# Two-layer diffusion backbone on one core: four outputs advance side by side over the k tiles at the start of each stage, and the second half's norm sums stand further on in PE's order

## The chip, the cores and the metric

One core of a Trainium2 chip runs the whole program in one launch. The metric is the device time of one execution in microseconds (us). A time is given as the median of several runs; a profile belongs to one execution and has that execution's own time.

## The reference

A trunk of two layers works on 512 latent tokens and 256 context tokens, 1024 channels each, in f32. Each layer is a half-step SwiGLU FFN, a token mixer, and another half-step FFN, and ahead of each stands a modulated RMS norm. Cut to what matters here:

```python
def rmsnorm(x, g):
    return x * lax.rsqrt(jnp.mean(x * x, axis=-1, keepdims=True) + EPS) * g
...
for l in range(DEPTH):                       # 2
    x = x + 0.5 * gate * ((silu(h @ wg) * (h @ wu)) @ wd)      # h = rmsnorm(x) * (1 + scale) + shift
    hx, hc = modulate(rmsnorm(x, ...)), modulate(rmsnorm(ctx, ...))
    yx, yc = even_mixer(hx, hc, ...) if l % 2 == 0 else odd_mixer(hx, hc, ...)
    x = x + mx[5] * yx
    x = x + 0.5 * gate * ((silu(h @ wg) * (h @ wu)) @ wd)
return rmsnorm(x, final_norm_g)
```

`shift`, `scale` and `gate` come from `silu(c) @ ada_w + ada_b`. The even mixer is a gated MLP beside windowed attention; the odd mixer is a convolution and a bidirectional recurrence with sigmoid gates.

## The kernel before, in words

**Layout.** Channels lie on the partitions, in 8 tiles of 128 ("the k tiles"), and the 768 tokens (256 context, then 512 latent) are columns. They are handled in two halves of 384 columns, TA (0 to 384) and TB (384 to 768); the last FFN has only latent tokens, in two halves XA and XB of 256. A weight is split into a high and a low part, and so is the normed input (`H`, tiles `hhi` and `hlo`): one product of f32 accuracy is three matmuls (`mm3`, L118). An output tile of 128 channels therefore costs 8 x 3 = 24 matmuls into one of 8 PSUM banks (`bank`, L105).

**A stage boundary.** The last thing that a stage does is to update X, channel tile by channel tile, first for TA and then for TB (`down` in `ffn`, L676, or `project_out`, L865). For each tile `Norm.add` (L548) squares the new X on ACT and DVE adds it to a sum (`flush`, L561). When all eight are in, `Norm.run` (L607) sets three things on a planner's clock: `stats` (L566, three matmuls with a column of ones, then a reciprocal square root of 13 small DVE instructions), then `spread` (L582, three matmuls that spread the result over the partitions), then for each k tile `apply` (L587: DVE multiplies, ACT adds the shift and writes `hhi`) and `halve` (L594: DVE writes `hlo`). PE's first products of the next stage read `hhi` and `hlo` of TA.

**The planner.** `Clock` (L72) is not the chip's time. Every `mm` adds an estimate to `clk.t` (L116: 173.5 ns for 384 columns), and `clk.tick()` after each `mm3` emits whatever has fallen due. So "2500 ns after" means "after the next 15 products in the program". The program order is then a priority: the framework issues an engine's instructions in that order when their inputs are expected, and may let a later one pass an earlier one that is not ready.

```python
        def run(self, after=2500.0):
            self.left = DK
            self.flush()
            clk.at(after, self._stats)

        def _stats(self):
            self.stats()
            self.prep_mod()
            clk.at(3600.0, self._spread)
```

`ready` (L624) runs the planner forward until all `halve` of a half have been emitted.

**The first products of a stage.** They go output by output, each over all 8 k tiles:

- `ffn`, `gate_up` (L653) for the first pair (p = 0): gate and up of f = 0, then of f = 1, for TA, and then the same for TB. In the first FFN the TA half is made earlier, in the start-up code (`pre`, L1389).
- `even_mixer`, `project_in` (L930): six outputs (two of k and v, four of q) for TA, called at L1127; those for TB are fillers between attention units.
- `odd_mixer`, `xx_mm` (L1257): four outputs for TA (L1356), then one of TB ahead of each `conv` (L1359).

Between stages weights are brought in by chunks (`Chunk`, L164): a DMA of 1 MB, a copy on ACT and a subtraction on DVE per tile (L189, L192; L219 and L236 in the FFNs that use a seven-product scheme). `stream["limit"]` bounds how many of the 12 weight tiles are planned at once; it is 8 from the end of an FFN until the second half's last `halve` (L603). In three FFNs DVE then forms sums of the `H` tiles (`form`, L701, `last_form`, L718) that the seven-product scheme reads from p = 2 (or 4) on.

**The modulation.** `ada_step` (L508) is a background job on DVE that multiplies `ada_w` with the condition. `ada_event` (L512) emits one step of it every 900 ns of the planner's clock until `mods[0][2]` is done, then less often. The end of one modulation is a small matmul on PE (`finish`, L463).

Of the kernel before, what the change touches and what calls it, by code (L numbers as in the profile page):

```python
# [89 lines left out]
def hybrid_kernel(ctx: ExitStack, tc: tile.TileContext, a: dict, out: bass.AP):  # L90
# [27 lines left out]
    def mm3(o, w, x, start, stop, again=False):  # L118

        mm(o, w[0], x[0], start, False, again=again)  # L120
        mm(o, w[0], x[1], False, False, again=again)
        mm(o, w[1], x[0], False, stop, again=again)
        clk.tick()

    def split(hi, lo, src, src_hi=None):
        act.activation(hi, src if src_hi is None else src_hi, AF.Copy)  # L126
# [385 lines left out]
    def ada_event():  # L512
        if bg["on"] and not (bg["sums"] and mods_done.get((0, 2), 0) == 4):
            ada_step()
        if not bg["over"]:
            clk.at(900.0 if mods_done.get((0, 2), 0) < 4 else bg["every"], ada_event)

    def mod(l, m):
        while mods_done.get((l, m), 0) < 4:
# [16 lines left out]
    class Norm:  # L536
# [67 lines left out]
                    stream["limit"] = SLOTS  # L604
                    pump()

        def run(self, after=2500.0):  # L607

            self.left = DK
            self.flush()  # L610
            clk.at(after, self._stats)

        def _stats(self):
            self.stats()
            self.prep_mod()
            clk.at(3600.0, self._spread)

        def _spread(self):
            self.spread()
# [23 lines left out]
    def ffn(l, j, halves, before, nxt, reserve=(), pre={}):  # L643
# [7 lines left out]
        with tc.tile_pool(name=f"ffn{l}{j}", bufs=4) as fp:  # L651

            def gate_up(p, spans, G):  # L653
                wg, wu = gu[p]
                need(wg)
                need(wu)
                for c0, c1 in spans:
                    n = c1 - c0
                    ready(c1, before)
                    if p == SEVEN.get((l, j), 99) - 2 and c1 == c_hi:  # L660
                        plan_forms(form, 4000.0 if p == 0 else 8000.0)
                    for f in (p, p + 1):
                        o = (f - p) * 128
                        made = (c0, f, 0) in pre
                        pg, pu = (pre[c0, f, i] if made else bank("pgu") for i in range(2))
                        for ps, w in ((pg, wg), (pu, wu)):
                            for k in range(0 if made else DK):
                                mm3(ps[:, 0:n], w.w(k, o, o + 128), (hi[k][:, c0:c1], lo[k][:, c0:c1]), k == 0, k == DK - 1)
                            if ps is pg:
                                s = temp("silu")[:, 0:n]  # L670
                                act.activation(s, pg[:, 0:n], AF.Silu)
                        g = temp("g")[:, 0:n]
                        dve.tensor_tensor(g, pu[:, 0:n], s, op=ALU.mult)
                        split(G[f][0][:, c0:c1], G[f][1][:, c0:c1], g)
# [211 lines left out]
    def even_mixer(before):  # L886
        hi, lo = H
        xd = dp.tile([128, 8, NT], F32, name="xd")
        with ExitStack() as es:
# [37 lines left out]
                return q_tiles[i // 2][:, i % 2]  # L927


            def project_in(i, c0, c1):  # L930
                ch = (ckv, cq[0], cq[1])[i // 2]
                need(ch)
                ps = bank()
                for k in range(DK):
                    w = ch.w(k, (i % 2) * 128, (i % 2) * 128 + 128)
                    mm3(ps[:, 0:c1 - c0], w, (hi[k][:, c0:c1], lo[k][:, c0:c1]), k == 0, k == DK - 1)
                act.copy(KV[:, i, c0:c1] if i < 2 else Q(i - 2)[:, c0:c1], ps[:, 0:c1 - c0])

            def rope(src):
                s_hi, s_lo = tr("sh", 2), tr("sl", 2)  # L940
# [182 lines left out]
                                      w[r, 0:256].rearrange("p (h t) -> p h t", h=2), op=ALU.mult)  # L1123

            ready(TA[1], before)
            for i in range(6):
                project_in(i, *TA)  # L1127
            kv = xp.tile([128, 4, NT], F32R, tag="x", name="kv")
            spare = xp.tile([128, 4, NT], F32R, tag="x", name="spare")
            keys(0, 2)  # L1130
# [24 lines left out]
            def fill_in(i):  # L1155

                if i < 6:
                    ready(NT, before)
                    project_in(i, *TB)
                    if i % 2:  # L1160
                        if i == 5:
                            stream["limit"] = SLOTS - 3
                        done((ckv, cq[0], cq[1])[i // 2])
                if i == 1:
                    rope(KV[:, 0, NCTX:])
                    keys(2, 6)
                elif i == 2:
                    values(3, 6)
                elif i > 2:
                    rope(Q(i - 3)[:, NCTX:])  # L1170
# [48 lines left out]
    def odd_mixer(before):  # L1219
# [4 lines left out]
        with tc.tile_pool(name="odd", bufs=1) as op:  # L1224
# [29 lines left out]
                area["xc"] = xp.tile([128, 4, NT], F32, tag="x", name="xc")  # L1254
                area["t0"] = xp.tile([128, 4, NT], F32, tag="x", name="t0")

            def xx_mm(k, c0, c1):  # L1257
                ch = cxx[k // 2]
                ready(c1, before)
                need(ch)  # L1260
                o = k % 2 * 128
                ps = xps[k, c0] = bank()
                for kk in range(DK):
                    mm3(ps[:, 0:384], ch.w(kk, o, o + 128), (hi[kk][:, c0:c1], lo[kk][:, c0:c1]), kk == 0, kk == DK - 1)
                if k % 2 and c0:
                    done(ch)

            def conv(k):

# [83 lines left out]
                gelu2(v, ps, 512)  # L1353
                combine(k, v)

            for k in range(4):  # L1356
                xx_mm(k, *TA)
            take()
            for k in range(4):  # L1359
                xx_mm(k, *TB)  # L1360
                conv(k)
                if k == 1:
                    halve_next(0)
            for k in range(8):
                do_rg(k)
                for kind, n in ODD_FILL[k]:
                    if kind == "xx":
                        xx_mm(n, *TA)
                        xx_mm(n, *TB)
                        conv(n)  # L1370
                    else:
                        do_gx(n)
# [189 lines left out]
```

## Time and profile before

| what | value |
|---|---|
| median of 3 runs | 2581.3 us (2578.44 to 2583.24) |
| the profiled execution's own time | 2580.57 us |
| its span, first to last instruction | 2578.8 us |
| mean granted TensorE clock | 0.988 |
| PE busy | 2522.0 us (98%) |
| DVE busy | 1883.5 us (73%) |
| ACT busy | 1247.0 us (48%) |

A row of the profile has a start and a duration in us from the span's start; "x24" counts instructions; square brackets give the idle time of the engine just before and what ended it. `ps<-hhi,w` reads "writes tile ps from hhi and w". The granted clock is 1.00 at 2.4 GHz and 0.50 at 1.2 GHz.

### The profile page before, as it was taken

To read this page: it belongs to the slowest core of one execution; us is meant where nothing else is said; L and a number is where in the kernel's file an instruction comes from. 1 tells how busy PE (TensorE), PEld (TensorE's weight loads), DVE (VectorE), ACT (ScalarE), POOL (GpSimd) and SP (SyncE) were. 2 spreads that over 40 slices of the span, in tenths; PEclk is the share of its full clock that TensorE was granted. 3 is DMA by queue.
4 is the path that set the end of the run, shared out by engine and by line. 5 is a ranking of instruction groups with operands and counts; after the bars stand their busy time and mean duration, and the time that the engine had idled before them with its cause. 6 is when DMAs were issued, how large, how long until landed. Compare 5 with 4: busy or idle time off the path is not lost.

```text
span 2578.8 us, 37727 instructions
## 1 busy us (share of the span) xinstructions
PE 2522.0 (98%) x14370; PEld 2354.4 (91%) x14370; DVE 1883.5 (73%) x3680; ACT 1247.0 (48%) x2433; POOL 210.2 (8%) x269
## 2 busy tenths in 40 slices
PE   8999999999999999999999999999999999999998
PEld 5999999998899999999899899999999989988887
DVE  7888977776879897786776988765468898644444
ACT  3344444445556354444454444444545996423322
POOL 0022012200000002201220021021200000000000
PEclk9999999999999999999999999999999999999999
DMA  9357558552112516645664176664642123322221
GB/s 329 107 139 180 146 133 207 144 164 93 34 58 56 184 57 156 175 121 136 166 169 151 46 186 170 200 148 106 139 131 82 51 81 104 110 98 98 90 90 58
DMA packets 248429, 328.45 MB, mean 127 GB/s; under 512 B 19984, under 2 KB 172728, under 8 KB 247736
## 3 DMA queue, kind: packets, MB, share of 16 engines
q1 hardware_dynamic: 213264, 278.69, 33.2%
q0 software_dynamic: 34560, 47.20, 12.1%
q8 instruction: 112, 1.84, 0.3%
q14 instruction: 69, 0.57, 0.1%
q10 hardware_dynamic: 424, 0.15, 0.0%
HBM read 262.04 MB, written 63.96 MB: 126 GB/s over the span
## 4 chain that ended last, share of the span: by engine, by line
PE 88%; DVE 6%; ACT 3%; DMA 2%; issue 1%; SPq 0%; ACTq 0%; DVEq 0%
PE pd L112 26%; PE pgu L112 25%; PE seeded L112 18%; PE ps L112 11%; PE po L112 4%; PE pv L112 2%; PE sc L112 1%; PE pt L1101 1%; PE sl L112 1%; DVE w L192 1%; PE pre L112 1%; DMA raw<-in_ffn_w_down_dram 1%; ACT w L189 1%; DVE hlo L598 0%; DMA fw<-in_ada_w_dram 0%
## 5 line engine op out<-in xcount | busy, mean ns | idle before, releaser
L112 PE MATMUL pd<-ghi,w 128*128 128x256 f32 (+2 forms) x2528 | 644.6, 342 | 2.1 <-ACT ghi L126 2.0
L112 PE MATMUL pgu<-hhi,w 128*128 128x384 f32 (+2 forms) x2144 | 596.1, 350 | 0.9 <-ACT hhi L592 0.6
L112 PEld LDWEIGHTS pd<-ghi,w 128*128 128x128 f32 x2528 | 439.3, 188 | 53.8 <-ACT ghi L126 4.9
L112 PE MATMUL pd<-glo,w 128*128 128x512 f32 (+2 forms) x1264 | 430.9, 342 | 0.2 <-DVE glo L127 0.2
L112 PEld LDWEIGHTS pgu<-hhi,w 128*128 128x128 f32 x2144 | 393.6, 189 | 27.9 <-ACT hhi L592 1.3
L112 PE MATMUL pgu<-hlo,w 128*128 128x384 f32 (+2 forms) x1072 | 375.1, 350 | 1.3 <-DVE hlo L598 1.2
L687 POOL DMA_DIRECT2D kept<-add x240 | 208.6, 905 | 1649.8 <-ACT add L686 1640.1
L192 DVE TENSOR_TENSOR w<-raw,w 128x512 fp32r<-128x512 f32 x404 | 271.3, 688 | 94.3 <-ACT w L189 91.6
L189 ACT ACTIVATE w<-raw 128x512 fp32r<-128x512 f32 x404 | 245.1, 626 | 176.5 <-PE pd L112 74.2
L487 DVE SCALAR_TENSOR_TENSOR acc<-aw,cs,acc 128x512 f32<-128x512 f32 x392 | 279.9, 746 | 46.0 <-DMA aw<-in_ada_w_dram 45.2
L219 DVE TENSOR_TENSOR w<-raw,w 128x512 fp32r<-128x512 f32 x348 | 232.9, 688 | 105.1 <-ACT w L236 101.2
L112 PE MATMUL seeded<-form,w 128*128 128x384 f32 x1392 | 263.0, 336 | 3.7 <-ACT seeded L780 2.6
L112 PEld LDWEIGHTS pd<-glo,w 128*128 128x128 f32 x1264 | 237.7, 188 | 27.0 <-DVE glo L127 2.7
L686 ACT ACTIVATE add<-pd,gate 128x256 f32<-128x256 f32 x240 | 138.8, 581 | 247.0 <-PE pd L112 226.6
L112 PE MATMUL seeded<-hhi,w 128*128 128x384 f32 x928 | 247.7, 335 | 1.5 <-ACT hhi L126 1.0
L112 PEld LDWEIGHTS seeded<-form,w 128*128 128x128 f32 x1392 | 244.0, 188 | 4.9 <-ACT seeded L780 2.9
L236 ACT ACTIVATE w<-raw 128x512 fp32r<-128x512 f32 x348 | 207.8, 626 | 59.9 <-DVE raw L235 18.9
L112 PEld LDWEIGHTS pgu<-hlo,w 128*128 128x128 f32 x1072 | 203.0, 189 | 15.1 <-DVE hlo L598 2.1
L112 PE MATMUL ps<-hhi,w 128*128 128x384 f32 (+1 forms) x704 | 198.4, 356 | 4.5 <-ACT t L1317 3.2
L112 PEld LDWEIGHTS seeded<-hhi,w 128*128 128x128 f32 x928 | 168.6, 188 | 3.4 <-ACT hhi L126 2.5
L112 PE MATMUL seeded<-hlo,w 128*128 128x384 f32 x464 | 155.3, 335 | 0.4 <-DVE hlo L127 0.4
L112 PEld LDWEIGHTS ps<-hhi,w 128*128 128x128 f32 x704 | 133.2, 194 | 11.6 <-ACT t L1317 3.8
(300 smaller groups left out, 3635.5 us busy)
## 6 DMA issues: line engine op xcount, KB each, us to landing
aw<-in_ada_w_dram SPq DMA_DIRECT2D x128, 512.0 KB, 5.2
raw<-in_ffn_w_gate_dram SPq DMA_DIRECT2D x44, 1024.0 KB, 5.4
raw<-in_ffn_w_up_dram SPq DMA_DIRECT2D x44, 1024.0 KB, 5.3
raw<-in_ffn_w_down_dram SPq DMA_DIRECT2D x40, 1024.0 KB, 5.1
kept<-add POOLq DMA_DIRECT2D x120, 256.0 KB, 5.3
kept<-add POOLq DMA_DIRECT2D x120, 128.0 KB, 5.3
x<-kept SPq DMA_DIRECT2D x48, 192.0 KB, 4.3
fw<-in_ada_w_dram SPq DMA_DIRECT2D x16, 512.0 KB, 8.8
```

The lines of the kernel that those rows point to most:

```text
L112: pe.matmul(o, w, x, start=start, stop=stop, skip_group_check=again)
L189: act.activation(tiles[i][:, 0:512], self.raw[:, i * 512:i * 512 + 512], AF.Copy)
L192: dve.tensor_tensor(t[:, 512:1024], self.raw[:, i * 512 - 512:i * 512], t[:, 0:512].bitcast(F32), op=ALU.subtract)
L219: dve.tensor_tensor(l, src[key], h.bitcast(F32), op=ALU.subtract)
L236: act.activation(halves_of(key)[0], src[key], AF.Copy)
L487: dve.scalar_tensor_tensor(acc[:, v, :], w[:, k, :], s, acc[:, v, :], op0=ALU.mult, op1=ALU.add)
L686: act.activation(t, ps[:, 0:c1 - c0], AF.Copy, scale=state["gate"][:, 4 * c + d, v:v + 1])
L687: pool.dma_start(out=saved(l, j)[:, 4 * c + d, c0:c1], in_=t, accum_op=ALU.add)
L1101: pe.transpose(ps[:, o:o + 128], self.src[hh][b + bb], ident)
```

## The change

The program has a new helper, `side_by_side`, which takes several outputs and loops over the k tiles outside and over the outputs inside. It is used for the first products of each stage: in the FFNs for the four outputs of p = 0, for each half that was not made in the start-up code; in the even mixer for the first four and then the last two outputs of TA; in the odd mixer for the four of TA and then for pairs of TB. So `conv(0)` comes after two outputs of TB. The number of products, their operands and each bank's order over k stay as they were.

`Norm.run` has other distances for the second half: `stats` after 5500 ns (3500 ns where a half is 256 wide) in place of 2500, and `spread` 3000 ns after that in place of 3600. The first half keeps its distances. `ada_event` has 800 ns in place of 900. In the even mixer the limit on weight tiles is raised after the first four outputs.

```diff
+    def side_by_side(parts, n, c0, c1):
+
+        for k in range(DK):
+            for o, w in parts:
+                mm3(o[:, 0:n], w(k), (H[0][k][:, c0:c1], H[1][k][:, c0:c1]), k == 0, k == DK - 1)
...
-            clk.at(900.0 if mods_done.get((0, 2), 0) < 4 else bg["every"], ada_event)
+            clk.at(800.0 if mods_done.get((0, 2), 0) < 4 else bg["every"], ada_event)
...
-        def run(self, after=2500.0):
+        def run(self):
...
-            clk.at(after, self._stats)
+            clk.at(2500.0 if self.c1 < NT else 5500.0 if self.n == 384 else 3500.0, self._stats)
...
-            clk.at(3600.0, self._spread)
+            clk.at(3600.0 if self.c1 < NT else 3000.0, self._spread)
...
+                    four = {}
+                    if p == 0 and (c0, p, 0) not in pre:
+                        four = {(f, i): bank("pgu") for f in (0, 1) for i in range(2)}
+                        side_by_side([(ps, lambda k, f=f, i=i: (wg, wu)[i].w(k, f * 128, f * 128 + 128)) for (f, i), ps in four.items()], n, c0, c1)
                     for f in (p, p + 1):
                         o = (f - p) * 128
-                        made = (c0, f, 0) in pre
-                        pg, pu = (pre[c0, f, i] if made else bank("pgu") for i in range(2))
+                        made = p == 0
+                        pg, pu = (pre[c0, f, i] if (c0, f, i) in pre else four[f, i] if four else bank("pgu") for i in range(2))
...
-            def project_in(i, c0, c1):
-                ch = (ckv, cq[0], cq[1])[i // 2]
-                need(ch)
-                ps = bank()
-                for k in range(DK):
...
+            def project_in(tiles, c0, c1):
+                pss, parts = {}, []
+                for i in tiles:
...
+                side_by_side(parts, c1 - c0, c0, c1)
+                for i, ps in pss.items():
+                    act.copy(KV[:, i, c0:c1] if i < 2 else Q(i - 2)[:, c0:c1], ps[:, 0:c1 - c0])
...
-            for i in range(6):
-                project_in(i, *TA)
+            project_in(range(4), *TA)
+            stream["limit"] = SLOTS
+            project_in((4, 5), *TA)
...
-            for k in range(4):
-                xx_mm(k, *TA)
+            xx_mm(range(4), *TA)
             take()
             for k in range(4):
-                xx_mm(k, *TB)
+                if k % 2 == 0:
+                    xx_mm((k, k + 1), *TB)
                 conv(k)
```

## Rows read from the trace of the kernel before

**Rows 1.** The page: PE's busy time, and the chain that ended last.

```profile
PE 2522.0 (98%) x14370; PEld 2354.4 (91%) x14370; DVE 1883.5 (73%) x3680; ACT 1247.0 (48%) x2433; POOL 210.2 (8%) x269
...
PE 88%; DVE 6%; ACT 3%; DMA 2%; issue 1%; SPq 0%; ACTq 0%; DVEq 0%
```

**Rows 2.** PE's waits, whole span: releaser, us in total, times, longest.

```profile
PE ps L112 <- DVE ssq L563: 4.4, 4, 1.6
...
PE ps L112 <- DVE red L497: 3.5, 1, 3.5
...
PE ps L112 <- DVE hlo L598: 2.2, 4, 0.6
...
PE ps L112 <- DVE rstd L144: 1.0, 1, 1.0
```

**Rows 3.** Stage starts: us, then busy (x instructions) of PE, PEld, DVE, ACT, POOL; PEclk.

```profile
578.95:588.69 9.74, 6.39 (x26) 4.21 (x25) 9.06 (x26) 5.84 (x15) 0.00 (x0) 0.78 0.26 89
588.69:597.00 8.31, 8.31 (x37) 8.31 (x37) 4.08 (x19) 0.39 (x2) 0.00 (x0) 0.64 0.96 298
597.00:613.75 16.75, 16.75 (x99) 16.72 (x98) 9.46 (x19) 7.06 (x16) 0.00 (x0) 1.00 0.11 33
1421.10:1430.17 9.07, 6.07 (x25) 4.09 (x25) 9.07 (x25) 4.42 (x10) 0.00 (x0) 0.85 0.53 181
1430.17:1439.00 8.83, 8.83 (x44) 8.83 (x45) 4.89 (x20) 1.19 (x3) 0.00 (x0) 0.76 0.01 3
...
1950.73:1960.37 9.64, 6.31 (x25) 4.19 (x24) 9.27 (x26) 6.17 (x16) 0.28 (x6) 0.80 0.46 152
1960.37:1969.00 8.63, 8.63 (x37) 8.63 (x38) 5.08 (x34) 1.03 (x2) 0.00 (x0) 0.63 0.59 195
...
899.06:910.00 10.94, 9.99 (x62) 9.67 (x62) 8.57 (x26) 4.25 (x7) 0.00 (x0) 1.00 0.41 134
110.00:122.00 12.00, 9.17 (x45) 9.17 (x46) 10.51 (x24) 5.78 (x13) 0.00 (x0) 0.86 0.28 84
```

**Rows 4.** PE's timeline, first half's sums and spread, then the even mixer's start.

```profile
563.34 0.72 PE L112 MATMUL ps<-ones,ssq 128*128 128x1 f32 x6
567.72 0.83 PE L112 MATMUL ps<-ident,rstd 128*128 128x128 f32 x6
...
588.69 1.44 PE L112 MATMUL ps<-ones,ssq 128*128 128x1 f32 x6 [1.58 <-DVE ssq L563]
```

**Rows 5.** DVE's timeline at the even mixer's start.

```profile
585.30 0.74 DVE L598 SCALAR_TENSOR_TENSOR hlo<-h,mods,hhi 128x256 fp32r<-128x256 f32 x2
...
588.08 0.56 DVE L563 TENSOR_TENSOR ssq<-ssq,sq 128x384 f32<-128x384 f32 x1 [0.56 <-ACT sq L557]
...
597.28 1.67 DVE L591 SCALAR_TENSOR_TENSOR h<-x,modA,ps 128x384 f32<-128x384 f32 x3 [3.37 <-PE ps L112]
```

**Rows 6.** DVE's timeline at the start of layer 1's first FFN.

```profile
1436.01 1.14 DVE L591 SCALAR_TENSOR_TENSOR h<-x,modA,ps 128x384 f32<-128x384 f32 x2 [2.03 <-PE ps L112]
...
1446.26 0.56 DVE L673 TENSOR_TENSOR g<-pgu,silu 128x384 f32<-128x384 f32 x1 [0.66 <-PE pgu L112]
```

**Rows 7.** The same FFN, windows after that start.

```profile
1439.00:1456.00 17.00, 17.00 (x100) 17.00 (x99) 16.19 (x33) 8.28 (x17) 0.00 (x0) 1.00 0.01 1
1456.00:1490.00 34.00, 32.28 (x166) 29.80 (x165) 33.11 (x66) 16.94 (x35) 0.00 (x0) 0.95 0.08 31
```

**Rows 8.** The odd mixer: windows once its recurrence runs.

```profile
1990.00:2000.00 10.00, 10.00 (x59) 10.00 (x59) 9.97 (x18) 9.87 (x18) 0.43 (x9) 1.00 0.22 71
2000.00:2060.00 60.00, 59.53 (x328) 57.31 (x327) 51.60 (x67) 56.84 (x83) 0.25 (x6) 1.00 0.18 54
```

**Rows 9.** DVE's timeline in the odd mixer: first applied tile, a convolution, the last split.

```profile
1969.01 0.61 DVE L591 SCALAR_TENSOR_TENSOR h<-x,modA,ps 128x384 f32<-128x384 f32 x1 [2.58 <-PE ps L112]
...
1983.06 0.75 DVE L1281 SCALAR_TENSOR_TENSOR xc<-xr,vecb,xc 128x512 f32<-128x512 f32 x1 [2.61 <-ACT xc L1279]
...
1992.51 0.95 DVE L127 TENSOR_TENSOR xl<-xc,xh 128x768 fp32r<-128x768 f32 x1
```

More of the change, by code (lines that the diff above doesn't have):

```diff
@@ L927, in Q @@
                 return q_tiles[i // 2][:, i % 2]
-            def project_in(i, c0, c1):
-                ch = (ckv, cq[0], cq[1])[i // 2]
-                need(ch)
-                ps = bank()
-                for k in range(DK):
-                    w = ch.w(k, (i % 2) * 128, (i % 2) * 128 + 128)
-                    mm3(ps[:, 0:c1 - c0], w, (hi[k][:, c0:c1], lo[k][:, c0:c1]), k == 0, k == DK - 1)
-                act.copy(KV[:, i, c0:c1] if i < 2 else Q(i - 2)[:, c0:c1], ps[:, 0:c1 - c0])
+            def project_in(tiles, c0, c1):
+                pss, parts = {}, []
+                for i in tiles:
+                    ch = (ckv, cq[0], cq[1])[i // 2]
+                    need(ch)
+                    pss[i] = bank()
+                    parts.append((pss[i], lambda k, ch=ch, o=(i % 2) * 128: ch.w(k, o, o + 128)))
+                side_by_side(parts, c1 - c0, c0, c1)
+                for i, ps in pss.items():
+                    act.copy(KV[:, i, c0:c1] if i < 2 else Q(i - 2)[:, c0:c1], ps[:, 0:c1 - c0])
             def rope(src):
@@ L1158, in fill_in @@
                     ready(NT, before)
-                    project_in(i, *TB)
+                    project_in((i,), *TB)
                     if i % 2:
@@ L1255, in take, with xx_mm @@
                 area["t0"] = xp.tile([128, 4, NT], F32, tag="x", name="t0")
-            def xx_mm(k, c0, c1):
-                ch = cxx[k // 2]
+            def xx_mm(ks, c0, c1):
                 ready(c1, before)
[L1260 to L1266, printed above, removed]
+                parts = []
+                for k in ks:
+                    ch = cxx[k // 2]
+                    need(ch)
+                    ps = xps[k, c0] = bank()
+                    parts.append((ps, lambda kk, ch=ch, o=k % 2 * 128: ch.w(kk, o, o + 128)))
+                side_by_side(parts, 384, c0, c1)
+                for k in ks:
+                    if k % 2 and c0:
+                        done(cxx[k // 2])
             def conv(k):
@@ L1367, in odd_mixer @@
                     if kind == "xx":
-                        xx_mm(n, *TA)
-                        xx_mm(n, *TB)
+                        xx_mm((n,), *TA)
+                        xx_mm((n,), *TB)
                         conv(n)
```

## The prediction

> **What bounds the kernel now.** I read the page first. PE is busy 98% of the span and makes 88% of the chain that ended last [rows 1], so time goes only where PE waits or runs slowly. Next came PE's waits [rows 2]: the sums of the second half's norm wait for DVE's `ssq`, the first products for `hlo`, and one early product 3.5 us for `red`. They look small. The windows of the stage starts [rows 3] show what they cost. From 597.00 on, the even mixer's last four outputs, 96 products, take 16.75 us: 0.1745 us each at full clock. The 18.05 us before hold two outputs, 48 products (8.4 us), and the norm's sums and spread, 1.2 us by the first half's rows at full clock (0.72 and 0.83 with their overlap taken off) [rows 4]. So 8.5 us are lost, part as idle time, part as products at a clock of 0.78 and 0.64 of full: the clock falls to 1.2 GHz after the waits. The other starts, counted the same way (the twelve small instructions and the edge ones taken off the counts): the odd mixer loses 18.27 - 49 x 0.1745 - 1.2 = 8.5 us, layer 1's first FFN 17.90 - 56 x 0.1745 - 1.2 = 6.9 us, layer 0's second FFN 10.94 - 50 x 0.1745 - 1.2 = 1.0 us. The window from 110 to 122, where PE waits for `red`, loses 12.0 - 43 x 0.1745 - 0.2 = 4.3 us. Together 29 us of 2578.8.
>
> Why PE waits: DVE is 9.06 us busy of the 9.74 at the even mixer's start [rows 3]. It updates TB, adds its squares and applies TA at once, and writes TA's last `hlo` only at 586.04 [rows 5]. One output wants a new k tile every 3 products, 0.52 us, and its eighth 3.7 us into the stage. Then the sums wait: `ssq` is complete at 588.64, 0.56 us of that waiting for ACT's last square [rows 5].
>
> **The change part by part.**
>
> *Four outputs side by side, TA.* Each k tile now carries 12 products, 2.09 us, so the eighth is wanted 14.6 us into the stage: at 593.6 in the even mixer, 7 us after it is written. The wait for `hlo` goes in all three starts. Nothing is added: the same matmuls, the same weight tiles. What must be there earlier is the second pair's weights, within the first 1.1 us; in the even mixer their subtractions lie before or just after the stage's start in the same DVE stretch, the tile for k = 6 and 7 needed only 12 us in. I cost them at nothing; without that cover it is one subtraction behind DVE's queue, 1 to 2 us.
>
> *Sums of TB later.* Planned 5500 ns on, they stand behind 33 products, 5.8 us into the stage; `ssq` is there 9.1 to 9.7 us in. As written PE would wait 3.5 us. But order in the program is not order on PE: before, the sums were planned after 15 products and stood behind 24, all that the one open bank had (x26 in the first window, less the two at its edges) [rows 3]. The framework lets products of banks already open pass sums that are not ready. Four open banks give 96 to pass with, so I expect the sums near product 50, at about 588, and no wait over 1 us. Bounds: no wait (0), or 3.9 us and a stretch at 1.2 GHz. I take 0.5 us per start, near the lower, because at layer 0's second FFN such a passing order ended in a wait of only 1.0 us at full clock [rows 2, 3].
>
> *Even mixer.* 8.5 saved less 0.5: **-8.0**. Behind it the rest of the mixer is PE's, at clock 1.00 in the window that follows and with DVE busy 9.46 of 16.75 us [rows 3], so the gain stays. Bounds -8.5 and -3.
>
> *Layer 1's first FFN.* Here the gain meets DVE. From 1439 to 1456 DVE is 16.19 us busy of 17, from 1456 to 1490 33.11 of 34, while PE already idles 1.7 us [rows 7]: the forms are what PE waits for next. Their work starts with the first applied tile of TB at 1436.01, after 2.03 us of idle waiting for the spread, and idles 0.66 us more at 1446.26 for a PE output [rows 6]. Earlier sums are impossible (`ssq` ends the same DVE queue); what is saved is the half-clock sums and spread, about 1.5 us, and the 0.66. **-2.2** of the 6.9; the other 4.7 becomes a longer wait of PE at the forms. Bounds -6.9 and 0.
>
> *Odd mixer.* PE comes to the first gate product 8.5 us earlier. Two things must follow. TB's first `apply` waits 2.58 us for the spread, which stood behind half-clock products [rows 9]; it moves about 3 us forward. The convolutions' DVE work, idle 2.61 us for ACT now, ends with the split at 1993.4 [rows 9], and `conv(0)`, put behind two outputs, loses nothing since `conv(1)` needed the second anyway. I count the split about 7 us earlier. From there ACT is the bound, 9.87 of 10 us, then 56.84 of 60 [rows 8]; its chain begins with the gate products, so it moves whole. **-7.0**; bounds -8.5 and -1, as in the FFN.
>
> *Layer 0's second FFN.* Sums planned 2.3 us later, the spread 3000 after: the spread comes out within 1 us of 909, the wait of 1.0 us may go or stay, and the forms on DVE follow it. **-0.3**; bounds -1.0 and +2.3. The last FFN has narrow halves, a wait of 0.3 us at most, and its sums 0.7 us later with the spread 0.6 us closer: **0**, bounds -0.3 and +0.7.
>
> *TB side by side, and evictions.* TB's four outputs want four banks when TA's four have just ended: eight, less four, less the spread's, leaves three. The fourth is wanted 1.57 us after TA's first output ends, whose Silu frees it sooner than that. But gate and up of both tiles end within 1.6 us of each other, and the tiles for the next step come in a burst. **+1.0** in all, bounds 0 and +5.
>
> *Background job at 800 ns.* The step count to `finish` is 41, so it stands 4.1 us, some 24 products, earlier, its DVE steps too; each waits for its `aw` load, issued on SP's queue behind weight loads. Both sides of the wait move together. **-0.5**, bounds -4.3 and +4.
>
> **The sum:** -8.0 - 2.2 - 7.0 - 0.3 + 0 + 1.0 - 0.5 = -17.0. The profiled execution took 2580.57 us, its span 2578.8 plus 1.8 around it, and the median is 0.7 above it: 2581.3 - 17.0 = **2564**.
>
> On the evictions the row and a rule speak differently. The next output's products run straight on now, an output's `g` taking 0.56 us beside them [rows 6]. The Trainium skill, Perfetto Trace Analysis, section Optimizing Tensor Performance (Matmuls), wants independent groups to rotate through PSUM banks so that the eviction of one overlaps the matmuls of the next; four groups that end together do that worse. If that rule decided, each of the five starts would pay what the third rival below prices. No row before has four groups ending together outside the start-up code, so the traces bear the rule out only weakly.
>
> **The rivals.**
>
> *1. The sums wait as planned.* PE stands at product 33 in the even and odd mixers until `ssq`, 3.5 us, and then loses what the second window of the even mixer's start loses now, 8.31 - 24 x 0.1745 - 1.2 = 2.9 us [rows 3]: 6.4 of 8.5 lost again, 2 saved in each, 2 in the FFN, the small terms +0.2: some 6 in all, 2575. For it: PE executes in order, and the order is fixed before the run. Against: the passing seen now.
>
> *2. The sums pass too far, and the sign turns.* Sums that are not ready may be passed by all 96 products of the open banks. Then TB's spread comes when TA is done, 17.9 us into the stage. The even mixer keeps its 8.0, covered by two more outputs. Layer 1's first FFN has its DVE chain start at 1439.0 in place of 1435.1, +3.9; layer 0's second at 917 in place of 909, +7.8; the odd mixer's TB products wait for eight tiles of `apply` and `halve`, 8.5 us, plus half clock: gain gone, +2. Sum +5.7: 2587. It decides from about product 65 on, where the FFN's chain starts as late as now. For it: the rule of passing. Against: in every start the sums ran as soon as `ssq` was there.
>
> *3. The burst of evictions.* Each of five starts waits for a Silu and a `g`, 1.1 us by 0.56 each [rows 6], twice over as TB and the step after it do the same, and loses half of that 2.9 us to the clock: 5 x 3.7 = 18 us, which eats the 18 that the rest of the sum saves: 2581.
>
> *4. The gain is absorbed downstream.* The odd mixer behaves like the FFN and returns 5 of its 7, the even mixer 4 of its 8 in its attention units: -8, 2573.
>
> **How the numbers follow.** A measurement of this kernel tells about 0.2%, 5.2 us, from no change. My forecast, 2556 to 2572: 0.57. Rivals 1 and 4, at 2575 and 2573: 0.12 each, within 2576. More than forecast (every bound at its best gives 2552): 0.04. Rival 3: 0.09, rival 2: 0.06. Faster takes the forecast, 1, 4 and the better end: 0.85, less 0.03 for those that end short of 5.2 us: 0.82. Same: rival 3 and the 0.03, less 0.02 of rival 3 that ends slower: 0.10. Slower: 0.08. The range 2556 to 2576 holds the forecast and rivals 1 and 4, 0.81.
>
> **What would show it.** Right: no idle PE time for `hlo` at 579 to 595, 1421 to 1435 and 1951 to 1967, the granted clock there 1.00, the sums near product 50 of the stage, TB's first apply 2 to 3 us earlier, and in layer 1's first FFN more idle PE time between 1456 and 1490 than now. Wrong: sums behind 33 products with a wait of 3 us (rival 1) or behind all 96 (rival 2); waits of `pgu` for Silu or `g` (rival 3); in the odd mixer longer waits for L1317 by as much as the start gained (rival 4).

## The result and the profile after

The changed kernel takes 2560.95 us (median of 6 runs, 2559.14 to 2565.06) against 2579.44 us for the kernel before (6 runs, 2575.30 to 2583.24): a ratio of 0.993, 95% interval 0.9917 to 0.9943. That is 18.5 us faster, beyond the 5.2 us that a measurement of this kernel can tell. The forecast was 2564.

The page, PE's busy time and the chain that ended last:

```profile
PE 2512.1 (98%) x14370; PEld 2347.8 (92%) x14370; DVE 1882.6 (74%) x3680; ACT 1242.0 (49%) x2432; POOL 210.2 (8%) x269
...
PE 73%; issue 14%; DVE 5%; ACT 3%; POOL 2%; DMA 2%; SPq 1%; POOLq 0%; ACTq 0%; DVEq 0%
```

PE has the same 14370 instructions and is 9.9 us less busy [rows 1]: products at half clock are booked as busy time, and there are fewer of them now. PE's waits, whole span (releaser, us in total, times, longest):

```profile
PE ps L112 <- ACT t L1332: 6.8, 2, 3.8
...
PE ps L112 <- DVE red L503: 2.8, 1, 2.8
...
PE pgu L112 <- ACT form L132: 1.8, 1, 1.8
```

The lines for `ssq`, `hlo` and `rstd` [rows 2] are gone. No wait of `pgu` for Silu or `g` has come. The same stretches from each stage's start as [rows 3] and, for the FFN, [rows 7]:

```profile
580.19:589.93 9.74, 9.74 (x58) 9.74 (x58) 9.52 (x26) 5.48 (x14) 0.00 (x0) 1.00 0.26 89
589.93:598.24 8.31, 8.31 (x53) 8.20 (x52) 6.11 (x23) 1.93 (x5) 0.00 (x0) 1.00 0.91 282
1414.95:1424.02 9.07, 9.07 (x54) 9.07 (x54) 9.07 (x25) 3.99 (x9) 0.00 (x0) 1.00 0.55 182
1424.02:1432.85 8.83, 8.68 (x55) 8.39 (x54) 5.73 (x21) 1.67 (x3) 0.00 (x0) 1.00 0.00 1
1432.95:1449.95 17.00, 17.00 (x100) 17.00 (x99) 17.00 (x35) 9.62 (x19) 0.00 (x0) 1.00 0.01 1
1449.95:1483.95 34.00, 29.69 (x142) 26.37 (x141) 32.87 (x67) 17.35 (x35) 0.00 (x0) 0.90 0.09 31
1942.19:1951.83 9.64, 9.64 (x57) 9.64 (x57) 9.52 (x26) 6.64 (x15) 0.28 (x6) 1.00 0.46 152
1951.83:1960.46 8.63, 8.63 (x56) 8.63 (x55) 7.57 (x41) 2.17 (x7) 0.00 (x0) 1.00 0.62 196
```

In the first 9.74 us of the even mixer PE makes 58 products without a gap at full clock; before it was 26 instructions at 0.78. All three starts look like that. In the sixth row the gain of the FFN's start turns up as loss: 4.3 us idle and a clock of 0.90, where the same stretch before had 1.7 us and 0.95.

Cut at marks that every trace has, the 18.3 us by which the span shrank lie here: start-up +1.2; even mixer -8.4 from its start to its first score product (`sc`), and +1.4 from there to its output's norm sums; layer 0's second FFN -0.4; layer 1's first FFN -2.4; odd mixer -8.9; last FFN -0.9.

PE's timeline has the second half's sums, one row each of the even mixer, layer 1's first FFN and the odd mixer:

```profile
590.07 0.72 PE L112 MATMUL ps<-ones,ssq 128*128 128x1 f32 x6
...
1425.01 0.72 PE L112 MATMUL ps<-ones,ssq 128*128 128x1 f32 x6
...
1952.25 0.72 PE L112 MATMUL ps<-ones,ssq 128*128 128x1 f32 x6
```

They stand behind 57, 58 and 58 products of the stage (24 before) and take 0.72 us, as at full clock in [rows 4], where one took 1.44. DVE's timeline in the FFN (the last square's addition, the first step after the sums, TB's first applied tile):

```profile
1423.42 0.55 DVE L569 TENSOR_TENSOR ssq<-ssq,sq 128x384 f32<-128x384 f32 x1
...
1425.77 0.16 DVE L143 TENSOR_SCALAR rs<-ps 128x3 f32<-128x3 f32 x1 [1.63 <-PE ps L112]
...
1429.20 1.66 DVE L597 SCALAR_TENSOR_TENSOR h<-x,modA,ps 128x384 f32<-128x384 f32 x3 [1.09 <-PE ps L112]
```

`ssq` is complete at 1423.97, the sums run 1.04 us later. TB's first tile is applied 14.25 us into the stage, 14.91 before [rows 6]; in the even mixer 15.5 and 18.3.

### The profile page after: what moved, and what is told of

Same layout as the page of the kernel before. It is cut to its first block, busy times and chain, and to the rows that moved or that the text cites. A ratio compares the mean times of both kernels' runs of the same rounds, so it can differ in the third digit from the quotient of the medians.

```text
span 2560.5 us, 37733 instructions
## 1 busy us (share of the span) xinstructions
PE 2512.1 (98%) x14370; PEld 2347.8 (92%) x14370; DVE 1882.6 (74%) x3680; ACT 1242.0 (49%) x2432; POOL 210.2 (8%) x269
## 4 chain that ended last, share of the span: by engine, by line
PE 73%; issue 14%; DVE 5%; ACT 3%; POOL 2%; DMA 2%; SPq 1%; POOLq 0%; ACTq 0%; DVEq 0%
PE pgu L112 21%; PE pd L112 20%; PE seeded L112 13%; PE ps L112 10%; PE po L112 4%; POOL kept L697 2%; PE pv L112 2%; PE sc L112 1%; PE pt L1113 1%; PE sl L112 1%; DMA kept<-add 1%; DVE form L709 1%; DMA kept<-x 0%; ACT w L195 0%; DMA aw<-in_ada_w_dram 0%
## 5 line engine op out<-in xcount | busy, mean ns | idle before, releaser
L112 PE MATMUL pd<-ghi,w 128*128 128x512 f32 (+2 forms) x2528 | 644.3, 342 | 2.3 <-ACT ghi L132 2.2
L112 PE MATMUL ps<-hhi,w 128*128 128x384 f32 (+1 forms) x704 | 191.8, 347 | 3.0 <-ACT t L1332 3.0
L112 PE MATMUL pgu<-form,w 128*128 128x384 f32 x696 | 134.7, 340 | 2.3 <-ACT form L132 1.8
```

The lines of the kernel that those rows point to most:

```text
L112: pe.matmul(o, w, x, start=start, stop=stop, skip_group_check=again)
```

## The experiments

Theory at the start: the loops side by side carry the gain, and the planned distance hardly matters. The rival: the later distance is needed. The table collects what the runs gave. The columns are: how many products of the stage stand ahead of the second half's sums (even mixer, layer 1's first FFN, odd mixer; as PE's order in the program has it); the even mixer from its start to its first score product; that FFN from its start to the first gate or up product after its first `down`; the odd mixer from its start to its output's norm sums; from the even mixer's start to the end, which leaves the start-up out; and the time (median, or the one run). All lengths are of the one profiled execution of a kernel.

| kernel | sums behind | even | FFN | odd | even start to end | time |
|---|---|---|---|---|---|---|
| before | 24, 24, 24 | 35.2 | 110.6 | 233.1 | 1999.8 | 2579.4 |
| after | 57, 58, 58 | 26.8 | 108.2 | 224.2 | 1980.3 | 2561.0 |
| e1, loops alone | 57, 58, 58 | 26.8 | 109.0 | 224.3 | 1981.1 | 2561.4 |
| e2, distances alone | 48, 48, 48 | 28.3 | 107.5 | 225.3 | 1980.6 | 2565.6 |
| e9a, 4100 and 4300 | 24, 24, 24 | 34.7 | 112.0 | 233.6 | 2000.8 | 2577.7 |
| e9b, 4250 and 4300 | 48, 48, 48 | 28.3 | 107.2 | 226.0 | 1982.5 | 2567.2 |
| e9c, 4250 and 3600 | 48, 48, 48 | 34.5 | 107.2 | 231.6 | 1996.3 | 2573.5 |
| e3, sums behind all | 102, 96, 96 | 27.8 | 115.8 | 232.2 | 2008.0 | 2590.3 |
| e6, two and two | 48, 48, 48 | 29.9 | 106.1 | 226.1 | 1984.1 | 2563.4 |
| e8, TB one by one | 57, 58, 58 | 26.8 | 108.0 | 224.1 | 1981.4 | 2560.0 |
| e5, 900 ns | 57, 58, 58 | 26.8 | 108.6 | 225.5 | 1983.6 | 2565.4 |
| e4, shorter forms | 57, 58, 58 | 26.8 | 103.7 | 224.2 | 1976.1 | 2559.3 |
| e7, forms later | 57, 58, 58 | 26.8 | 102.0 | 224.1 | 1978.8 | 2560.4 |
| e7 again | 57, 58, 58 | 26.8 | 102.0 | 222.6 | 1977.6 | 2559.3 |

### e1: the loops alone

```diff
-            clk.at(2500.0 if self.c1 < NT else 5500.0 if self.n == 384 else 3500.0, self._stats)
+            clk.at(2500.0, self._stats)
...
-            clk.at(3600.0 if self.c1 < NT else 3000.0, self._spread)
+            clk.at(3600.0, self._spread)
...
-            clk.at(800.0 if mods_done.get((0, 2), 0) < 4 else bg["every"], ada_event)
+            clk.at(900.0 if mods_done.get((0, 2), 0) < 4 else bg["every"], ada_event)
```

> Only the loops side by side; the distances of sums and spread (2500 and 3600 ns) and the background job's 900 ns are those of the kernel before. In this program's instruction order the sums stand behind 57, 58 and 58 products in the even mixer, layer 1's first FFN and the odd mixer, exactly as in the changed kernel, since the framework passes sums that are not ready; only in layer 0's second FFN are they 13 products earlier. Theory (the side-by-side loops carry the gain, the planned distance hardly matters): even mixer's start to its first score product 26.8 us as in the changed kernel (35.2 before), odd mixer 224 us from its start to its output's sums (233 before), layer 1's first FFN 108 us from its start to the first product of its second weight round (110.6 before); total 2561, within 2 us of the changed kernel. Rival 1 (the later distance is needed): PE stands 3.5 us for ssq early in each stage and about 6 us of the gain are left in all, 2571 to 2576.

Measured: 2561.4 us (5 runs, 2559.73 to 2563.07), ratio to before 0.9929 (0.9917 to 0.9941). The whole gain is there without the new distances. The rival falls, and with it the prediction's first: PE does not stand at product 15, where the plan has the sums, because in PE's order they stand behind 57.

### e2: the distances alone

```diff
         def run(self):
...
-            clk.at(after, self._stats)
+            clk.at(2500.0 if self.c1 < NT else 5500.0 if self.n == 384 else 3500.0, self._stats)
...
-            clk.at(3600.0, self._spread)
+            clk.at(3600.0 if self.c1 < NT else 3000.0, self._spread)
...
             for i in range(6):
+                if i == 4:
+                    stream["limit"] = SLOTS
                 project_in(i, *TA)
```

> Only the distances of the second half's sums and spread (5500 or 3500 and 3000 ns); products output by output as before, one bank after the other, 900 ns. (The limit on weight tiles is raised after the even mixer's fourth output, as in the changed kernel, since otherwise a chunk would come too late for its use.) The sums stand behind 48 products, two outputs, in the three starts (24 before, 57 with the change). Theory: the waits for hlo stay, about 1.8 us at a start, and the half clock behind them; the wait for ssq, 1.6 us, goes. Even mixer and odd mixer about 3 us shorter each, layer 1's first FFN between 0 and 2.5 us longer, because its spread and with it the DVE chain comes later: total 2575, between 2571 and 2579. Rival (the later sums carry half of the gain or more): 2570 or less.

Measured: 2565.6 us (6 runs, 2557.69 to 2567.71), ratio 0.9942 (0.9929 to 0.9956). My theory fell: from the even mixer's start to the end the profiled execution is within 0.3 us of the changed kernel's, without one loop side by side. The windows of its even and odd starts, and PE's only wait left there:

```profile
575.26:585.00 9.74, 8.51 (x50) 8.18 (x49) 9.08 (x26) 6.23 (x16) 0.00 (x0) 1.00 0.26 89
585.00:593.31 8.31, 8.31 (x52) 8.31 (x53) 6.58 (x24) 2.53 (x6) 0.00 (x0) 1.00 0.93 290
1936.15:1945.79 9.64, 8.51 (x50) 8.20 (x49) 9.30 (x26) 6.20 (x18) 0.28 (x6) 1.00 0.48 152
1945.79:1954.42 8.63, 8.63 (x54) 8.63 (x55) 8.03 (x42) 3.20 (x5) 0.00 (x0) 1.00 0.59 195
```

```profile
PE ps L112 <- DVE ssq L563: 3.2, 4, 1.2
```

The waits for `hlo`, which I had left to the loops, are gone too. PE's order in the program shows why (A, B: the first two outputs' banks; the digit is the k tile; x3 means three products):

```
before: A0x3 A1x3 A2x3 A3x3 A4x3 A5x3 A6x3 A7x3 | sums | B0x3 ...
e2:     A0x3 A1x3 A2x3 A3x3 A4x3 A5x1 B0x3 B1x3 B2x1 A5x2 B2x2 B3x3 A6x1 B4x3
        A6x2 B5x2 A7x1 B5x1 B6x3 B7x1 A7x2 B7x2 | sums
```

With two banks open the framework itself puts B's ready products in front of A's that still wait for `hlo`. Before, B's products could not come at all until the sums were through, although they had no need of the sums. New theory: banks are given out in program order, so a small step planned inside output A holds back the bank of every output that opens after it.

The times say less than this profile, which is of the lowest of the six runs. Two runs took 2557.7 and 2558.7 us, with a mean granted clock of 0.994; the other four took 2565.1 to 2567.7 with 0.991, and have no trace. By the median the distances alone bring 13.9 us, where the loops alone bring 18.1. The 0.003 of clock over 2560 us is about 7.7 us (an estimate; as the clocks are rounded, 5 to 10), about as much as the four are longer, so the lower clock can account for it. Where it was lower is not seen. The wait of 1.24 us for `ssq` that this kernel keeps is one candidate: in e6 the clock fell after a wait of that size. The changed kernel has no such wait.

### e9a and e9b: 150 ns of the plan

```diff
-            clk.at(after, self._stats)
+            clk.at(4100.0 if self.c1 == NT and self.n == 384 else 2500.0, self._stats)
...
-            clk.at(3600.0, self._spread)
+            clk.at(4300.0 if self.c1 == NT and self.n == 384 else 3600.0, self._spread)
```

The second kernel has 4250.0 for 4100.0; both have e2's line for the limit on weight tiles.

> The kernel before with one distance changed: in the second halves of 384 columns the sums are planned 4100 ns on and the spread 4300 after that (the limit on weight tiles is raised in the even mixer as in the changed kernel). 4100 ns end with product 24 at the latest, so the sums come in the program after the first output's last product and ahead of the second output's first. Theory (PSUM banks are given out in program order: the second output's bank comes after the sums' bank, so none of its products may start before the sums): sums behind 24 products as in the kernel before, PE waits for hlo and for ssq, granted clock near 0.78 and 0.64 at the even mixer's start; even mixer's start to first score product 35 us, odd mixer to its sums 232 to 234, total 2576 to 2584. Rival (a later place in the plan helps by degrees): 15 products before, 24 here, 33 in the run with distances alone, so about half of its 14 us, 2572.

> The same kernel with 4250 ns in place of 4100: 150 ns of the plan, less than one product. The sums now come in the program behind the second output's first product, so its bank is given out before theirs. Theory: both banks' products stand ahead of the sums, in the order in which their hlo tiles are there, 48 in all; no wait for hlo at the three starts, at most 1.2 us for ssq, clock 1.00; even mixer's start to first score product 28.3 us, odd mixer to its sums 225, layer 1's first FFN 107.5, total 2566, within 5 us. Rival (by degrees): as with 4100 ns, 2572 or more.

The even mixer's start with 4100, and PE's waits:

```profile
575.16:584.90 9.74, 6.07 (x27) 4.28 (x27) 9.45 (x26) 5.85 (x15) 0.00 (x0) 0.92 0.26 89
584.90:593.21 8.31, 8.31 (x39) 8.31 (x39) 3.70 (x19) 0.94 (x3) 0.00 (x0) 0.68 0.97 295
```

```profile
PE ps L112 <- DVE ssq L563: 4.6, 4, 1.6
...
PE ps L112 <- DVE hlo L598: 2.7, 4, 0.8
```

And with 4250:

```profile
582.87:592.61 9.74, 8.51 (x50) 8.18 (x49) 9.08 (x26) 6.22 (x16) 0.00 (x0) 1.00 0.29 89
592.61:600.92 8.31, 8.31 (x52) 8.31 (x53) 6.58 (x24) 2.53 (x6) 0.00 (x0) 1.00 0.94 292
```

4100 ns give the kernel before, 4250 ns the kernel with the gain: less than one product in the plan, and 18.3 us from the even mixer's start to the end (2000.8 against 1982.5). The times alone show 10.6 us of it, since the second execution's start-up happened to be 7.7 us longer. Nothing goes by degrees between the two; what decides is whether the sums or the second output's first product stand first in the program. That it is the bank which holds the second output back is the theory that forecast both, and e9c below; no run gave the sums a bank outside the common pool.

### e9c: the spread ahead of the third output

```diff
-            clk.at(4300.0 if self.c1 == NT and self.n == 384 else 3600.0, self._spread)
+            clk.at(3600.0, self._spread)
```

> The run with 4250 ns once more, with the spread 3600 ns behind the sums, as in the kernel before, in place of 4300. Then the spread falls due at product 48 at the latest, ahead of the third output's first product, and its bank comes ahead of the third output's. Theory (a small step's bank holds back every output that opens later in the program): nothing stands between sums and spread, 24 products with 4300 ns; PE waits some 4 us for rstd, a wait that no kernel of this study has shown at a start, and then runs some us at half clock. Even mixer's start to first score product 33 to 36 us (28.3 with 4300 ns), odd mixer to its sums 230 to 233 (226), total 2578, between 2573 and 2583: 700 ns of the plan cost what the better place of the sums had brought. Rival (only the sums' place matters): 2567, no wait for rstd.

The even mixer's start, PE's first wait by size, and PE's timeline there:

```profile
575.41:585.15 9.74, 8.52 (x49) 8.19 (x48) 9.05 (x26) 6.22 (x16) 0.00 (x0) 1.00 0.26 89
585.15:593.46 8.31, 4.46 (x19) 4.38 (x20) 6.04 (x23) 2.00 (x5) 0.00 (x0) 0.66 0.93 286
```

```profile
PE ps L112 <- DVE rstd L144: 11.4, 4, 3.8
```

```profile
585.16 0.83 PE L112 MATMUL ps<-ones,ssq 128*128 128x1 f32 x6 [1.23 <-DVE ssq L563]
589.82 1.65 PE L112 MATMUL ps<-ident,rstd 128*128 128x128 f32 x6 [3.83 <-DVE rstd L144]
```

As expected: nothing stands between the sums and the spread, PE idles 3.83 us, and the spread itself runs at half clock (1.65 us for 0.83). A wait of that size was not new, as the expectation has it: e3, below, shows one of 4.1 us. The theory holds for a second step. In the even and odd mixers that costs 6.2 and 5.6 us; in the FFN nothing, where DVE is waited for anyway.

### e3: the sums behind all products

```diff
-            clk.at(2500.0 if self.c1 < NT else 5500.0 if self.n == 384 else 3500.0, self._stats)
+            clk.at(2500.0 if self.c1 < NT else 17500.0 if self.n == 384 else 3500.0, self._stats)
```

> The changed kernel with the second half's sums planned 17500 ns on where halves are 384 wide, so that they stand behind all 96 (even mixer 102) products of the first half. This forces the case of my rival 2 and tests its price. Theory: the even mixer keeps its start (26.8 us to the first score product, within 1.5 us, as two more outputs cover the spread), and the three others wait for the spread with nothing left to do: layer 0's second FFN +8 us, layer 1's first FFN +6 to +10, odd mixer +11 against the changed kernel; total 2587, between 2583 and 2595. Rival (PE has enough other work and DVE is late anyway): 2575 or less.

Measured: 2590.3 us, slower than the kernel before. The even mixer keeps its start; layer 0's second FFN loses 10.1 us against the changed kernel, layer 1's first 7.6, the odd mixer 8.0. PE's wait by size, and the window of layer 0's second FFN in which it falls:

```profile
PE ps L112 <- DVE rstd L150: 10.0, 3, 4.1
```

```profile
910.00:925.00 15.00, 9.59 (x45) 9.21 (x44) 9.07 (x27) 6.44 (x11) 0.00 (x0) 0.77 0.00 0
```

So the later place that brings the gain has an upper end, and the second rival's price, 2587, was about right; of its parts, the odd mixer came out better than priced (0.9 us under the kernel before, where +2 was said) and the FFNs worse. How far past 58 products the turn lies was not tried.

### e6: two pairs in place of four

```diff
-            project_in(range(4), *TA)
+            project_in((0, 1), *TA)
+            project_in((2, 3), *TA)
...
-            xx_mm(range(4), *TA)
+            xx_mm((0, 1), *TA)
+            xx_mm((2, 3), *TA)
```

In the FFNs the pairs are gate and up of f = 0, then of f = 1.

> The changed kernel with the first half's four outputs taken in two pairs, side by side within a pair. Each k tile then carries 6 products, 1.05 us, and the eighth is wanted 7.3 us into the stage, when DVE has just written it; the sums stand behind 48 products, 8.4 us in, and ssq is there 9.0 us in. Theory: two open banks are enough; no wait for hlo, one of 0.6 to 1.2 us for ssq at each of the three starts, clock 1.00. Even mixer's start to first score product 27.5 to 28.3 us (26.8 with four), odd mixer to its sums 225, layer 1's first FFN 107.5 because its sums come about 1 us earlier; total 2562, between 2559 and 2566. Rival (four are needed, since a wait of this size halves the clock): 3 us more at each of the three starts, 2569 or more.

Measured: 2563.4 us. The sums wait 1.24, 0.59 and 1.12 us. The even mixer's start and its sums:

```profile
577.48:587.22 9.74, 8.50 (x50) 8.19 (x49) 9.09 (x26) 6.23 (x16) 0.00 (x0) 1.00 0.26 89
587.22:595.53 8.31, 8.31 (x43) 8.31 (x44) 4.99 (x21) 0.96 (x3) 0.00 (x0) 0.79 0.92 288
```

```profile
587.21 0.83 PE L112 MATMUL ps<-ones,ssq 128*128 128x1 f32 x6 [1.24 <-DVE ssq L569]
```

Two open banks are enough for `hlo`. The even mixer missed its bound (29.9 for at most 28.3): its clock fell after the wait. In layer 1's first FFN TB's first tile is applied 13.3 us into the stage in place of 14.25 and the start to the second round is 2.2 us shorter: what comes earlier on DVE seems to count there, and e4 tests it.

### e4: what layer 1's first FFN waits for

```diff
                 whole(r, k + 4, R)
-                dve.tensor_tensor(p, p, q, op=ALU.subtract)
-                dve.tensor_tensor(q, q, r, op=ALU.subtract)
                 split(F3[:, k], F3[:, 4 + k], q)
```

> The changed kernel with two of the nine DVE operations of each form left out (the two subtractions; the sums that the seven-product scheme reads are then others), 8 x 0.55 = 4.4 us of DVE time in each of the three FFNs that have forms. Theory (layer 1's first FFN gave back most of its start's gain because DVE, 32.9 of 34 us busy, is what PE waits for at the forms): its start to its second round's first product shrinks from 108.2 us by 3 to 6 (4.4 us of DVE and some of the half clock), while layer 0's second FFN, where PE does not wait for the forms, changes by less than 0.7 us. Rival (the gain was lost to something else there, weights or ACT): less than 1 us in both.

Measured: 2559.3 us. The window that answers to the changed kernel's sixth:

```profile
1451.74:1485.74 34.00, 30.78 (x169) 28.70 (x168) 33.70 (x68) 18.27 (x37) 0.00 (x0) 1.00 0.17 58
```

169 products in place of 142, the clock at 1.00, and 4.55 us less to the second round, for 4.4 us of DVE left out. DVE is the bound there. Layer 0's second FFN, from its first half's norm sums to its second round, changed by -1.1, more than the 0.7 allowed; but with e3 left out it varies from 124.2 to 127.1 us between the traces (e2 and e9b, with whole forms, have 124.6 and 124.2), so nothing follows from that.

### e7: a version that starts the forms later

```diff
-SEVEN = {(0, 0): 4, (0, 1): 2, (1, 0): 2}
+SEVEN = {(0, 0): 4, (0, 1): 2, (1, 0): 4}
```

> A try at a faster version: the changed kernel with layer 1's first FFN using the seven-product scheme from p = 4 on, as layer 0's first FFN does, and not from p = 2. One pair of outputs more by ordinary products costs 24 products, 4.2 us; its 192 products give DVE 33 us more for the forms, so PE's 4.3 us of idle time from 1450 to 1484 and the half clock there (0.90 of 34 us, 3.4 us) go. Theory: start to second round 108.2 us -2 (between -4 and +2), total 2559, between 2556 and 2563. Rival (weights come late, or the idle time was for something other than the forms): 2565.

> The version with the seven-product scheme from p = 4 on in layer 1's first FFN once more, for its time alone: its profile showed that FFN 3.5 us shorter than in the changed kernel (523.8 against 527.2 us from its start to the odd mixer's), its five runs a median only 0.6 us lower. Theory: 3 us less, 2558, and that FFN again 523 to 525 us. Rival (what is saved there is lost elsewhere): 2561.

The same window:

```profile
1451.34:1485.34 34.00, 34.00 (x200) 34.00 (x200) 20.77 (x41) 12.61 (x26) 0.00 (x0) 1.00 0.13 34
```

PE does not wait at all now, and DVE is 20.8 us busy. That FFN takes 523.8 and 524.5 us from its start to the odd mixer's, 527.2 in the changed kernel. The medians are 2560.4 (5 runs, ratio to before 0.9932, 0.9918 to 0.9947) and 2559.3 (6 runs, 0.9924, 0.991 to 0.9938), all eleven 2559.5: 1.5 us under the changed kernel's, within what the measurement tells from none.

### e8 and e5: the small terms

e8: the odd mixer's TB outputs one at a time, and `four` in the FFNs only for the first half.

```diff
-                    if p == 0 and (c0, p, 0) not in pre:
+                    if p == 0 and (c0, p, 0) not in pre and c0 < c_hi - n:
...
-                        made = p == 0
+                        made = (c0, f, 0) in pre or bool(four)
...
-                if k % 2 == 0:
-                    xx_mm((k, k + 1), *TB)
+                xx_mm((k,), *TB)
```

> The changed kernel with the second half's outputs one by one again (in the FFNs gate and up of f = 0, then of f = 1; in the odd mixer one output ahead of each convolution), the first half's four side by side. This measures the prediction's term for side-by-side outputs of TB and their evictions, +1.0 with bounds 0 and +5. Theory: the term is 0, no wait for Silu or g shows with four together and the framework lets products pass one another anyway: even mixer and both FFNs within 0.7 us of the changed kernel, odd mixer to its sums 224 us within 0.7, total 2561, within 4 us. Rival 1 (the burst of evictions costs): layer 1's first FFN or the odd mixer 1 us or more shorter here. Rival 2 (one output of TB at a time wants its k tiles faster than DVE writes them): 1 to 3 us longer in layer 1's first FFN.

Measured: FFN -0.3, odd mixer -0.2, even mixer 0.0 against the changed kernel, 2560.0 us. Neither rival shows: the term is 0 for TB's outputs. For TA's four, which stay side by side here, the traces show no wait of `pgu` for Silu or `g`.

e5:

```diff
-            clk.at(800.0 if mods_done.get((0, 2), 0) < 4 else bg["every"], ada_event)
+            clk.at(900.0 if mods_done.get((0, 2), 0) < 4 else bg["every"], ada_event)
```

> The changed kernel with the background job's 900 ns in place of 800. Term of the prediction: the 800 ns save 0.5 us (bounds 4.3 and -4), so this run takes 2561.5, and the wait for red at the end of the first modulation is 3.5 us again (2.8 with 800 ns). The changed kernel reached the even mixer 1.2 us later than the kernel before (580.2 against 579.0): if the 800 ns cost that in the start-up code, this run's even mixer starts at 579.0 and it takes about 2560; if that is the spread between executions (the first loads), it starts anywhere between 578.5 and 580.5.

Measured: 2565.4 us, even mixer's start at 580.05: with 900 ns it comes as late as in the changed kernel, so the 800 ns do not explain that. The wait for `red` was 4.1 us; but with 900 ns it was 3.3 in e1, 4.3 in e9b and 1.8 in e2, and 2.8 with 800 ns lies among them. Of the 3 us or so that this run is longer, 2.7 fall between the even mixer's first score product and its output's sums, in a stretch where executions of any of the kernels differ:

```profile
640.00:675.00 35.00, 32.53 (x186) 29.26 (x185) 28.78 (x78) 17.70 (x58) 0.00 (x0) 0.80 0.13 35
```

In the changed kernel the same stretch has 0.90 and 204 products. The background job's term stays unsettled: e1, with 900 ns, is 0.4 us from the changed kernel, this run 4.4 us.

## Why the prediction was right, and where not

**The loss at the starts: right.** 8.5, 6.9 and 8.5 us were counted as lost to waits and half clock. The even mixer's start got 8.4 back, the odd mixer's 8.9.

**Who brings it back: wrong.** The prediction let the loops remove the wait for `hlo` ("one output wants a new k tile every 3 products") and the distances the wait for the sums, as two parts of one sum. They are two ways to the same thing: in the profiled executions each alone brings 18.7 (e1) and 19.2 (e2) of the 19.5 us from the even mixer's start to the end, and the distances add 0.8 us to the loops, less than executions differ. Only in the medians are the distances alone behind, as said at e2. One output at a time was not what the loops before imposed; it came from the sums, which stood in the program ahead of the second output (e9a, e9b). The total did not suffer, since the loss of a start was counted once, for both parts together. That it came within 3 us is in part luck: the terms are off by +1.0 (even mixer), -1.9 (odd mixer), -0.9 (last FFN), -1.0 (evictions) and, for the start-up, +1.2, and these partly cancel. The passing itself was read rightly from the x26: sums that are not ready are passed by products of open banks. It was not followed to its other half, that banks which open later are held. The Trainium skill, PSUM — Partial Sum Buffer, section Engine vs sequencer instructions, says that matmuls start and complete in program order; the traces agree, for PE waits 3.83 us in front of the spread in e9c while 96 products that need no spread stand behind it. The passing is all in the order made before the run.

**Sums near product 50, no wait over 1 us: nearly.** 57 and 58, and no wait: in the FFN they run 1.04 us after `ssq` is there. The 0.5 us per start that were taken for a wait did not fall due.

**Layer 1's first FFN, -2.2: right,** -2.4, and for the reason given: the rest turned into PE's wait at the forms (4.3 us idle), and DVE time taken away there comes back one for one (e4). The idle 0.66 us and the cheaper sums do not make it up alone; the first tile came only 0.7 us earlier. In the mixers it came nearly 3 us earlier, as said.

**Odd mixer, -7.0: under-sized by 1.9.** The split on DVE moved from 41.8 to 34.0 us into the stage, 7.7 where 7 was counted, and the end of the stage moved by 8.9. The prediction took the split for what moves the rest; PE's own work does. PE's first gate product, which reads `xh`, stands behind the same 204 instructions of the stage in both kernels. It moved from 43.24 to 34.66 us into the stage, by 8.6, and PE comes to it without idling, before and after. First the kernel before (a window, the first gate product), then the changed kernel:

```profile
1969.00:1994.00 25.00, 25.00 (x146) 25.00 (x146) 22.27 (x42) 16.68 (x32) 0.34 (x6) 1.00 0.14 43
```

```profile
1993.97 0.33 PE L112 MATMUL ps<-xh,w 128*128 128x384 f32 x1
```

```profile
1960.46:1976.85 16.39, 16.39 (x96) 16.39 (x95) 16.19 (x30) 13.26 (x29) 0.34 (x6) 1.00 0.01 1
```

```profile
1976.85 0.33 PE L112 MATMUL ps<-xh,w 128*128 128x384 f32 x1
```

Rival 4 (gain absorbed) falls there. Its sign was longer waits for ACT's `t` by as much as the start gained. These waits come to 6.8 us after the change and to 6.3 before it:

```profile
PE ps L112 <- ACT t L1317: 6.3, 3, 3.1
```

**Even mixer, -8.0:** -8.4 at its start, +1.4 behind. The same stretch behind the first score product is between 260.9 and 265.0 us in these traces, before and after, so I put the 1.4 down to the spread between executions; that is argued, not shown.

**Evictions, +1.0: 0** (e8), and no wait in the trace. The rule of the Trainium skill (Perfetto Trace Analysis, Optimizing Tensor Performance, Matmuls) on rotating through PSUM banks did not decide: four groups that end together cost nothing that these runs show. Rival 3 falls.

**Last FFN, 0: -0.9,** outside its bounds of -0.3 and +0.7. Only the idle 0.3 us had been priced there. With the old distances and the loops (e1) 0.8 of it is there already.

**Start-up, not in the sum: +1.2.** The even mixer's start lies anywhere between 575.2 and 582.9 us in these traces, with no order by kernel. The six runs of e2 differ by 10 us, and its profiled one is the lowest, with one of the shortest start-ups (575.3); part of what its four higher runs lose may lie in the start-up.

## What to carry to other kernels

Where buffers are given out in program order, ask of each small step not only when it will be ready but whose buffer comes after its own: a step planned a moment too early can hold back work that has nothing to do with it. In such a kernel it pays to open the next independent output before the step (two open outputs removed the wait for the operand tiles here, four the wait for the step as well), and it turns sign when the step stands behind everything that could cover it. Compare stages between marks of the trace when executions differ by more than the effect.

## What was not expected of the hardware

A wait of 1.24 us of PE at the same place had two outcomes: the granted clock stayed at 1.00 after it in e2 and e9b, and fell to 0.79 over the next 8.3 us in e6, which cost 1.6 us. The start-up differed by up to 7.7 us between executions of programs that hardly differ there.
